# Elementwise x·y with GELU on one core: two 64 KB-row stretches of DRAM in place of three uneven ones, and the opening loads split by operand

## The chip, the cores and the metric

The kernel runs on one core of a Trainium2 chip. The metric is device time in microseconds (us) of one execution; the number for a kernel is the median of its runs.

## The reference

```python
batch, dim = 1024, 4096            # x and y, float32, 16.8 MB each
z = x * y
out = 0.5 * z * (1 + np.tanh(np.sqrt(2 / np.pi) * (z + 0.044715 * z ** 3)))   # float32
```

So 33.55 MB are read, 16.78 MB are written, and each element takes one multiplication and one GELU in its tanh form.

## The kernel before

The work is elementwise, so any element may lie in any partition. The kernel views x, y and out each as one flat run and cuts it into three stretches, `PIECES` (line 14), counted in columns of a 128-partition tile: 0 to 1280, 1280 to 17664, and 17664 to 32768. Inside a stretch, partition p owns one contiguous row of DRAM. A row of the first stretch is 5120 bytes, one of the second 65,536 bytes, and one of the third 60,416 bytes. The whole of x stays in SBUF as `xs` (32,768 columns); products and results are written over it in place. y goes through a smaller buffer `ys` of 20,440 columns, in three loads (`Y_LOADS`, line 16: the first and last column, and where it begins in `ys`).

Every transfer covers 128 partitions and so gives 128 rows, eight to each of the core's 16 DMA engines. In what follows the transfers of before are called by stretch and operand: xA and yA are the 5 KB-row ones, xB and yB the 64 KB-row ones, xC and yC the 60,416-byte ones.

The order in time is written by hand with semaphores:

- SyncE (SP) issues xA and ScalarE (ACT) issues xB. `_hoist` (line 25) puts both issues into the program's first block, ahead of each engine's first drain.
- SP then waits until xA has landed (line 81) and issues yB and xC one after the other.
- SP waits for multiplication 3 (`sem_mul`, line 86), which frees the part of `ys` that yC needs, and issues yC; it waits for multiplication 4 and issues yA.
- VectorE (DVE) multiplies (line 99): four steps of 4096 columns on stretch B, seven of 2048 and one of 768 on stretch C, one of 1280 on stretch A. Ahead of each stretch it waits for x and y of that stretch.
- ScalarE runs one GELU for each multiplication, as soon as that is done (line 107).
- SP issues three stores (line 116): B, after yC has landed (line 114) and the GELUs of B are done; C after the GELUs of C; A after the last GELU.
- Last, SP waits for the first two stores, clears the semaphores and waits for the third (lines 118 to 122).

SP's DMAs go through one queue (q1 in the profile) and ScalarE's through another (q10); both are worked off by the same 16 DMA engines.

Of the kernel before, what the change touches and what calls it, by code (L numbers as in the profile page):

```python
# [1 line left out]

# [4 lines left out]


F32 = mybir.dt.float32
GELU = mybir.ActivationFunctionType.Gelu_apprx_tanh  # L10

PIECES = [(0, 1280), (1280, 17664), (17664, 32768)]

Y_LOADS = [(1280, 17664, 4056), (17664, 32768, 0), (0, 1280, 15104)]

Y_FREE = [0, 3, 4]

STEPS = [[4096] * 4, [2048] * 7 + [768], [1280]]  # L20
STORES = [(1280, 17664), (17664, 32768), (0, 1280)]
Y_BUF = 20440


def _hoist(nc, issued):

    here = nc.cur_bb.bb.instructions
    first = nc.main_func.blocks[0].instructions
    for ins in issued:
        del here[next(k for k, i in enumerate(here) if i is ins or i.name == ins.name)]  # L30
    engine = issued[0].engine
    at = next(
        k
        for k, i in enumerate(first)
        if i.engine == engine and type(i).__name__ == "InstDrain"
    )
    first[at:at] = issued


@with_exitstack  # L40
def kernel(
    ctx: ExitStack,
    tc: tile.TileContext,
    x: bass.AP,
    y: bass.AP,
    out: bass.AP,
):
    nc = tc.nc
    P = nc.NUM_PARTITIONS

    def columns(t, a, b):

        flat = t.flatten_outer_dims().rearrange("r c -> (r c)")
        pa, pb = next(q for q in PIECES if q[0] <= a and b <= q[1])
        return flat[P * pa : P * pb].rearrange("(p c) -> p c", p=P)[:, a - pa : b - pa]


    tc.close()
    tc.compile()

    xs = nc.alloc_sbuf_tensor("xs", [P, PIECES[-1][1]], F32).ap()
    ys = nc.alloc_sbuf_tensor("ys", [P, Y_BUF], F32).ap()
    sem_x = [nc.alloc_semaphore(f"sem_x{i}") for i in range(len(PIECES))]
    sem_y = [nc.alloc_semaphore(f"sem_y{i}") for i in range(len(Y_LOADS))]
    sem_mul = nc.alloc_semaphore("sem_mul")
    sem_act = nc.alloc_semaphore("sem_act")
    sem_o = [nc.alloc_semaphore(f"sem_o{i}") for i in range(len(STORES))]

    def load_x(i, engine=nc.sync):
        a, b = PIECES[i]  # L70
        return engine.dma_start(out=xs[:, a:b], in_=columns(x, a, b)).then_inc(sem_x[i], 16)

    def load_y(i):
        a, b, r = Y_LOADS[i]
        return nc.sync.dma_start(
            out=ys[:, r : r + b - a], in_=columns(y, a, b)
        ).then_inc(sem_y[i], 16)

    _hoist(nc, [load_x(0).ins])
    _hoist(nc, [load_x(1, nc.scalar).ins])  # L80
    nc.sync.wait_ge(sem_x[0], 16)
    load_y(0)
    load_x(2)
    for i in range(1, len(Y_LOADS)):
        if Y_FREE[i]:
            nc.sync.wait_ge(sem_mul, Y_FREE[i])
        load_y(i)

    nc.scalar.wait_ge(sem_x[0], 16)
    n = 0  # L90
    done = {}
    for i, (a, b, r) in enumerate(Y_LOADS):
        for j, (xa, xb) in enumerate(PIECES):
            if xa <= a < xb:
                nc.vector.wait_ge(sem_x[j], 16)
        nc.vector.wait_ge(sem_y[i], 16)  # L96
        c = a
        for w in STEPS[i]:
            nc.vector.tensor_mul(  # L99
                out=xs[:, c : c + w],  # L100
                in0=xs[:, c : c + w],
                in1=ys[:, r + c - a : r + c - a + w],
            ).then_inc(sem_mul, 1)
            n += 1
            done[c + w] = n
            nc.scalar.wait_ge(sem_mul, n)
            nc.scalar.activation(  # L107
                out=xs[:, c : c + w], in_=xs[:, c : c + w], func=GELU
            ).then_inc(sem_act, 1)
            c += w  # L110

    for i, (a, b) in enumerate(STORES):
        if i == 0:
            nc.sync.wait_ge(sem_y[-2], 16)
        nc.sync.wait_ge(sem_act, done[b])
        nc.sync.dma_start(out=columns(out, a, b), in_=xs[:, a:b]).then_inc(sem_o[i], 16)
    for i in range(len(STORES) - 1):
        nc.sync.wait_ge(sem_o[i], 16)
    nums = sorted(s.num for s in [*sem_x, *sem_y, *sem_o[:-1], sem_mul, sem_act])
    assert nums == list(range(nums[0], nums[-1] + 1))  # L120
    nc.sync.sem_clear(range(nums[0], nums[-1] + 1))
    nc.sync.wait_ge(sem_o[-1], 16).then_inc(sem_o[-1], -16)


# [1 line left out]
_INS = ['x', 'y']  # L126
_OUTS = [((1024, 4096), 'float32')]


# [23 lines left out]
```

## Time and profile before

| What | Value |
|---|---|
| Median of 3 runs | 119.82 us (119.6 to 119.83) |
| Profiled execution, first to last instruction (its span) | 118.52 us |
| Median less that span | 1.30 us |
| DVE busy | 35.2 us (30% of the span) |
| ACT busy | 30.9 us (26%) |
| DMA queue q1 (SP), share of 16 engines | 82.3% |
| DMA queue q10 (ACT), share of 16 engines | 16.5% |
| Bytes read and written | 33.55 MB and 16.78 MB, 425 GB/s over the span |

The profile gives the profiled execution's own time as its span; what lies around the span in a timed run is the 1.30 us of the third row. The trace also lists every DMA packet with its start, its duration, its queue and its bytes. A row of a transfer is one packet there, and a 4-byte packet that follows a transfer's rows on an engine is that engine's report to the semaphore.

### The profile page before, as it was taken

The numbers are of one execution on the slowest core, as the hardware profiler recorded it, in microseconds if no ns is written. First come the engines' busy times: TensorE is split into PE (matmuls) and PEld (weight loads), VectorE is DVE, ScalarE is ACT, GpSimd is POOL, SyncE is SP. The second block draws the span as 40 slices with busy tenths as digits, with TensorE's granted clock in tenths as the row PEclk, the third lists the DMA queues.
The fourth block names the chain that finished last, engine by engine and source line by source line (L and its number), as shares of the span: only waits on it lengthen the run. The fifth ranks groups of instructions, "written<-read, shape, count | busy, mean of one in ns | idle before, by whom it ended". The sixth has DMA issues, their size and how long they took to land.

```text
span 118.5 us, 83 instructions
## 1 busy us (share of the span) xinstructions
DVE 35.2 (30%) x13; ACT 30.9 (26%) x14; POOL 0.2 (0%) x4
## 2 busy tenths in 40 slices
DVE  0000000000000069999920000059999940000000
ACT  0000000000000000999975000006998990000000
POOL 0000000000000000000000000000000000000000
DMA  9888899889988897798797797798899887977975
GB/s 492 382 382 382 354 597 464 354 354 465 597 354 354 354 632 347 326 632 347 326 632 347 326 632 347 326 575 354 354 531 531 354 354 326 653 326 326 653 326 221
DMA packets 1296, 50.33 MB, mean 425 GB/s; under 512 B 144, under 2 KB 144, under 8 KB 528
## 3 DMA queue, kind: packets, MB, share of 16 engines
q1 hardware_dynamic: 1152, 41.94, 82.3%
q10 hardware_dynamic: 144, 8.39, 16.5%
HBM read 33.55 MB, written 16.78 MB: 425 GB/s over the span
## 4 chain that ended last, share of the span: by engine, by line
DMA 55%; DVE 24%; ACT 3%; issue 1%; DVEq 0%
DMA ys<-in_y_dram 43%; DVE xs L99 24%; DMA xs<-in_x_dram 11%; ACT xs L107 3%; DVEq L96 0%
## 5 line engine op out<-in xcount | busy, mean ns | idle before, releaser
L99 DVE TENSOR_TENSOR xs<-xs,ys 128x2048 f32<-128x2048 f32 (+3 forms) x13 | 35.2, 2778 | 60.9 <-DMA ys<-in_y_dram 60.9
L107 ACT ACTIVATE xs<-xs 128x2048 f32<-128x2048 f32 (+3 forms) x13 | 29.6, 2300 | 19.6 <-DVE xs L99 19.6
L107 ACT ACT_TABLE_LOAD x1 | 1.3, 1283 | 47.2 <-DVE xs L99 47.2
L137 POOL MEMSET const-uint8-127<- 128x1 uint8 x1 | 0.1, 102 | 0.0
L137 POOL MEMSET const-bfloat16-1.0<- 128x1 bf16 x1 | 0.1, 101 | 0.0
L137 POOL MEMSET const-float32-0.0<- 128x1 f32 x1 | 0.1, 98 | 0.2 <-issue 0.2
L137 POOL MEMSET const-float32-1.0<- 128x1 f32 x1 | 0.1, 98 | 0.0
## 6 DMA issues: line engine op xcount, KB each, us to landing
xs<-in_x_dram SPq DMA_DIRECT2D x1, 7552.0 KB, 46.5
ys<-in_y_dram SPq DMA_DIRECT2D x1, 7552.0 KB, 22.5
out_dram<-xs SPq DMA_DIRECT2D x1, 7552.0 KB, 20.4
xs<-in_x_dram SPq DMA_DIRECT2D x1, 640.0 KB, 13.6
ys<-in_y_dram SPq DMA_DIRECT2D x1, 640.0 KB, 19.7
out_dram<-xs SPq DMA_DIRECT2D x1, 640.0 KB, 20.8
xs<-in_x_dram ACTq DMA_DIRECT2D x1, 30.4
ys<-in_y_dram SPq DMA_DIRECT2D x1, 29.0
```

Of the source, the lines that this page charges most:

```text
L99: nc.vector.tensor_mul(out=xs[:, c : c + w], in0=xs[:, c : c + w], in1=ys[:, r + c - a : r + c - a + w],).then_inc(sem_mul, 1)
L107: nc.scalar.activation(out=xs[:, c : c + w], in_=xs[:, c : c + w], func=GELU).then_inc(sem_act, 1)
L137: nc = _bacc.Bacc("TRN2", target_bir_lowering=False, num_devices=1)
```

## The change

- The flat run is cut into two stretches of 16,384 columns; every DRAM row is 64 KB apart from the next. Call the transfers x0, x1, y0, y1, y2, o0 and o1.
- SP opens with x0 (8.4 MB, 64 KB rows) and ScalarE with y0 (the same size). Both are hoisted. SP issues x1 right behind, without a wait.
- y's second half comes as y1, 12,288 columns (48 KB of each row), after multiplication 3, and y2, 4096 columns (16 KB of each row), after multiplication 4.
- DVE works in four steps of 4096 and eight of 2048 columns, twelve in place of thirteen.
- There are two stores: o0 after y1 has landed and the first four GELUs are done, o1 after the last GELU. Ahead of clearing the semaphores SP also waits for y2.
- ScalarE no longer waits for the first piece of x (line 89 of before).

```diff
-PIECES = [(0, 1280), (1280, 17664), (17664, 32768)]
+HALF = 16384
-Y_LOADS = [(1280, 17664, 4056), (17664, 32768, 0), (0, 1280, 15104)]
+Y_LOADS = [(0, 16384, 4056), (16384, 28672, 0), (28672, 32768, 12288)]
-Y_FREE = [0, 3, 4]
-STEPS = [[4096] * 4, [2048] * 7 + [768], [1280]]
-STORES = [(1280, 17664), (17664, 32768), (0, 1280)]
+STEPS = [[4096] * 4, [2048] * 6, [2048, 2048]]
...
-        pa, pb = next(q for q in PIECES if q[0] <= a and b <= q[1])
-        return flat[P * pa : P * pb].rearrange("(p c) -> p c", p=P)[:, a - pa : b - pa]
+        h = a // HALF * HALF
+        return flat[P * h : P * (h + HALF)].rearrange("(p c) -> p c", p=P)[:, a - h : b - h]
...
     _hoist(nc, [load_x(0).ins])
-    _hoist(nc, [load_x(1, nc.scalar).ins])
-    nc.sync.wait_ge(sem_x[0], 16)
-    load_y(0)
-    load_x(2)
-    for i in range(1, len(Y_LOADS)):
-        if Y_FREE[i]:
-            nc.sync.wait_ge(sem_mul, Y_FREE[i])
-        load_y(i)
+    _hoist(nc, [load_y(0, nc.scalar).ins])
+    load_x(1)
+    nc.sync.wait_ge(sem_mul, 3)
+    load_y(1)
+    nc.sync.wait_ge(sem_mul, 4)
+    load_y(2)
 
-    nc.scalar.wait_ge(sem_x[0], 16)
...
-        for j, (xa, xb) in enumerate(PIECES):
-            if xa <= a < xb:
-                nc.vector.wait_ge(sem_x[j], 16)
+        nc.vector.wait_ge(sem_x[a // HALF], 16)
         nc.vector.wait_ge(sem_y[i], 16)
...
-    for i, (a, b) in enumerate(STORES):
-        if i == 0:
-            nc.sync.wait_ge(sem_y[-2], 16)
+    nc.sync.wait_ge(sem_y[1], 16)
+    for i in range(2):
+        a, b = i * HALF, (i + 1) * HALF
         nc.sync.wait_ge(sem_act, done[b])
         nc.sync.dma_start(out=columns(out, a, b), in_=xs[:, a:b]).then_inc(sem_o[i], 16)
-    for i in range(len(STORES) - 1):
-        nc.sync.wait_ge(sem_o[i], 16)
-    nums = sorted(s.num for s in [*sem_x, *sem_y, *sem_o[:-1], sem_mul, sem_act])
+    nc.sync.wait_ge(sem_o[0], 16)
+    nums = sorted(s.num for s in [*sem_x, *sem_y, sem_o[0], sem_mul, sem_act])
...
+    nc.sync.wait_ge(sem_y[2], 16)
     nc.sync.sem_clear(range(nums[0], nums[-1] + 1))
-    nc.sync.wait_ge(sem_o[-1], 16).then_inc(sem_o[-1], -16)
+    nc.sync.wait_ge(sem_o[1], 16).then_inc(sem_o[1], -16)
```

## The prediction, made blind

> **What bounds the kernel now.** The page's busy times come first: no compute engine is busy for a third of the span, so they bound nothing by their sum.
>
> ```profile
> ## 1 busy us (share of the span) xinstructions
> DVE 35.2 (30%) x13; ACT 30.9 (26%) x14; POOL 0.2 (0%) x4
> ```
>
> Next the windows view, cut where the first DMA packet starts and where the last one ends; its last two columns are the mean busy share of the 16 DMA engines and GB/s.
>
> ```profile
> 0.00:1.00 1.00, 0.00 (x0) 0.00 (x0) 0.20 (x4) 1.00 0.00 0
> 1.00:118.13 117.13, 35.21 (x13) 30.90 (x14) 0.00 (x0) 1.00 1.00 430
> 118.13:118.52 0.39, 0.00 (x0) 0.00 (x0) 0.00 (x0) 1.00 0.00 0
> ```
>
> Between 1.00 and 118.13 us the DMA engines are full. So the chain of waits, which names DVE for 24% of the span, misleads here: while it follows DVE, other rows move. Only three things can change the time: how long the rows take, holes between them, and the 1.01 us before and 0.39 us behind them.
>
> The packet list, followed on one DMA engine, shows rows back to back; a short extract (start us, ns, queue, bytes):
>
> ```
> 1.119 216 q1 5120
> 2.506 2620 q10 65536
> 5.120 196 q1 5120
> 5.315 2418 q10 65536
> 12.947 2422 q10 65536
> 15.366 2418 q10 65536
> 17.780 2418 q1 65536
> 20.194 2418 q10 65536
> ```
>
> From it come the prices, start to start: 2.414 us for a 64 KB load row (17.780 to 20.194), 2.227 for a 60,416-byte one (yet eight of them go from 41.935 to 59.749), 0.193 for a 5 KB one. For stores on that engine: 2.426 (eight from 79.110 to 98.525), 2.231 (eight to 116.377), 0.205 (eight to 118.016). Two queues with rows waiting alternate one row at a time.
>
> Where the holes could come from is in the timeline and in SP's waits:
>
> ```profile
> 42.66 17.43 DVE L99 TENSOR_TENSOR xs<-xs,ys 128x4096 f32<-128x4096 f32 x4 [42.66 <-DMA ys<-in_y_dram]
> 55.79 4.66 SPq L75 DMA_DIRECT2D ys<-in_y_dram  x2
> 78.27 19.77 SPq L116 DMA_DIRECT2D out_dram<-xs  x3
> 78.34 17.78 DVE L99 TENSOR_TENSOR xs<-xs,ys 128x2048 f32<-128x2048 f32 x9 [18.25 <-DMA ys<-in_y_dram]
> ...
> 93.88 3.80 ACT L107 ACTIVATE xs<-xs 128x2048 f32<-128x2048 f32 x3 [0.29 <-DVE xs L99]
> ```
>
> ```profile
> SPq L116 <- DMA ys<-in_y_dram: 14.5, 1, 14.5
> ```
>
> yC is issued at 55.79 while xC still moves until 60, so nothing is lost there. Store B waits 14.5 us for yC, is issued at 78.27, and its first rows start at 79.11, at least 0.84 us later; what covers that is yA's 1.54 us alone. By the packet list nine of the 16 engines run dry here, for 0.1 to 0.5 us; the mean over the engines (yA's ends at 79.04, the store's starts at 79.17) is 0.13 us.
>
> **The change part by part.** The sum is made in DMA time of one engine, of the profiled execution (118.52 us); 1.30 us around the span, from the median 119.82, is carried over.
>
> Rows. Before: 16 rows of 5 KB at 0.193 (3.09), 16 of 64 KB at 2.414 (38.62), 16 of 60,416 at 2.227 (35.63), stores 8 × (2.426 + 2.231 + 0.205) = 38.90; sum 116.24. After: 24 load rows of 64 KB (57.94); y1's 48 KB rows lie on the line between 0.193 and 2.227, 1.812 each (14.50); y2's 16 KB rows by that line 0.607 (4.86); 16 store rows of 64 KB (38.82); sum 116.12. Gain 0.12 us. The bytes are the same; what goes is the part of a row's cost that doesn't shrink with it.
>
> The hole at 79 us. y2 now lasts 8 × 0.607 = 4.9 us, against 0.84 to 0.93 us from the issue of o0 to its rows. Gain 0.13 us on the mean engine. The slowest engine had none, so the bounds are 0 and 0.13; I take 0.13, since the engines' finishes close up during the stores (0.6 us apart at yA's landing, 0.2 at the last store's).
>
> The start. Before, the five 5 KB rows ahead of ScalarE's first row took 1.31 us on the mean engine (first starts at 1.12, that row at 2.43) instead of 5 × 0.193 = 0.97: 0.34 lost. ScalarE's first row took up to 2.858 us, 2.58 in the mean, 0.16 over a later one. After, one first row of 64 KB runs while all others queue. No such row opens before; the nearest is ScalarE's first, 0 to 0.44 over. I take 0.30 as its loss, a gain of 0.50 − 0.30 = 0.20, between 0 and 0.50.
>
> The end. The last report is 0.12 us behind the median engine's with 5 KB rows at the end (118.37, 118.48), and 0.22 with 64 KB rows (store B: 98.95, 99.16). I take 0.07 lost, between 0 and 0.10.
>
> The moved steps, each costed at nothing with its cover:
> - x0 and y0 alternate, so y0 is done after 16 rows: 1.12 + 0.30 + 38.62 = 40.0, landed by 40.4, against 42.57 before. DVE starts 2 us earlier, which by itself is worth nothing.
> - y1 waits for multiplication 3 and is in SP's queue ahead of y2 and o0. 13.1 us behind DVE's start is 53.5, plus at most 2.1 us to its first row (ScalarE's first, issued at 0.12, started at 2.23) is 55.6; x1's rows last until 59.4. Cover 3.8 us; beyond that each late microsecond costs one. y2 follows at 57.8, 16 us ahead of its turn.
> - o0 is issued when y1 lands, about 74.1, behind y2 in the queue, whose rows end at 78.8. Its GELUs are done by 62.
> - o1 waits for the last GELU: DVE from 74.2, eight steps at 2.20 (ACT's start-to-start in the timeline) to 91.8, the GELU behind by 2.2: 94.0. Its rows are needed at 98.2, cover 3.3 us after issue (before, 96.55 plus 0.9 against 98.6).
> - ScalarE's dropped wait and the added wait for y2 at the end stand beside 14 us and 38 us of idle time; nothing is queued behind the latter but the clear, itself 19 us early.
>
> Sum: −0.12 − 0.13 − 0.20 + 0.07 = −0.38, a span of 118.14 and a time of 119.45 us. Outer bounds of the main case: no start or hole gain and a full loss at the end, −0.02 (119.80); all of both and no loss at the end, −0.75 (119.07).
>
> **The rivals.** (1) The start-up gain isn't there: the engines lose the same 0.50 us. Then −0.18, 119.64, within what a measurement of this kernel can tell from no change (about 0.2%, 0.24 us). For it: the excess may be DRAM's first answers, whoever asks.
>
> (2) Slower: a 64 KB opening row comes later than a 5 KB one. SP's 5 KB row started 1.01 us behind its issue, ScalarE's 64 KB row 2.11 us. If the row's size makes that difference, x0 starts 1.1 us later and nothing covers it: 119.45 + 1.1 = 120.55. Against: store B's 64 KB rows came 0.84 us behind their issue, and exactly five 5 KB rows ran ahead of ScalarE's on the mean engine, which looks like rows already taken up. It decides from a first packet later than 1.4 us. [...]
>
> (3) Slower by far: SP's queue gets ahead. x1 now stands right behind x0; if an engine took all 16 of SP's rows first, y0 would end with x1 at 59.4, multiplication 3 at 72.7, y1's rows would come at 73.6, and 14 us of empty DMA would make 133.5. It decides once y0 is over 3.8 us late, two rows. Against: from 13 to 30 us the two queues alternate row by row. [...]
>
> **How the numbers follow.** Main case (start-up gain, over 0.2%) 0.50; rival 1 0.24; rival 2 0.20; rival 3 0.04; anything else slower 0.02. So faster 0.50, same 0.24, slower 0.26. The range goes from 119.15, nearly the main case's best, to 120.55, rival 2; it leaves out rival 3 and the outermost tails. The main case with rival 1 alone is 119.15 to 119.75.
>
> **What would show it.** Right: first packets at 1.0 to 1.4; y0 landed near 40.4 and DVE starting there; rows alternating q1, q10 from the second or third on; no engine idle near 79; o1 issued near 94, landed near 118.1. Wrong: a first packet near 2 us (rival 2), y0 landing at 45 or later (rival 3), idle DMA behind x1 or ahead of o1, or 64 KB rows longer than 2.42 us when both queues read.

## The result, and the profile after

| | Before | After |
|---|---|---|
| Median | 119.77 us (119.6 to 119.83, 4 runs) | 121.09 us (120.83 to 121.13, 4 runs) |
| Span of the profiled execution | 118.52 us | 119.75 us |

The ratio is 1.0107, with a 95% interval of 1.0093 to 1.0121. The change makes the kernel 1.1% slower, 1.3 us. The forecast was 119.45 us, in a range up to 120.55, with slower at 0.26.

The page's busy times, and the windows view cut as the one of before at the first packet's start and the last one's end (last two columns: DMA share, GB/s):

```profile
DVE 35.1 (29%) x12; ACT 31.0 (26%) x13; POOL 0.2 (0%) x4
```

```profile
0.00:1.00 1.00, 0.00 (x0) 0.00 (x0) 0.20 (x4) 1.00 0.00 0
1.00:119.40 118.40, 35.14 (x12) 31.03 (x13) 0.00 (x0) 1.00 1.00 425
119.40:119.76 0.36, 0.00 (x0) 0.00 (x0) 0.00 (x0) 1.00 0.00 0
```

The DMA engines are as full as before (share 1.00), yet carry 425 GB/s in place of 430. Nothing waits for data more than it did (VectorE 57.9 us in all, before 60.9); some packets take longer. So the shares of busy time can't show the loss, and the packet list must.

The timeline after:

```profile
0.00 1.90 SPq L68 DMA_DIRECT2D xs<-in_x_dram  x2
...
41.66 17.43 DVE L91 TENSOR_TENSOR xs<-xs,ys 128x4096 f32<-128x4096 f32 x4 [41.66 <-DMA ys<-in_y_dram]
...
54.79 4.67 SPq L72 DMA_DIRECT2D ys<-in_y_dram  x2
...
75.29 20.10 SPq L108 DMA_DIRECT2D out_dram<-xs  x2
75.37 17.71 DVE L91 TENSOR_TENSOR xs<-xs,ys 128x2048 f32<-128x2048 f32 x8 [16.27 <-DMA ys<-in_y_dram]
...
93.11 1.91 ACT L99 ACTIVATE xs<-xs 128x2048 f32<-128x2048 f32 x1 [0.29 <-DVE xs L91]
```

DVE starts at 41.66 (forecast 40.4), the first store o0 is issued at 75.29 (74.1), and the last GELU ends at 95.0 (94.0). In SP's waits the one of the first store for y is still there:

```profile
SPq L108 <- DMA ys<-in_y_dram: 12.5, 1, 12.5
```

All this is far enough ahead of its use. The windows around the end of the loads show what is not as planned:

```profile
74.10:76.60 2.50, 1.23 (x1) 0.00 (x0) 0.00 (x0) 1.00 1.04 439
76.60:77.90 1.30, 1.30 (x2) 0.21 (x1) 0.00 (x0) 1.00 1.19 365
77.90:79.30 1.40, 1.40 (x1) 1.40 (x1) 0.00 (x0) 1.00 0.79 199
79.30:80.80 1.50, 1.50 (x2) 1.21 (x2) 0.00 (x0) 1.00 2.01 863
```

A packet is counted in the window in which it starts, so single figures swing: the last line has the starts of o0's 64 KB rows. The share counts packets in the same way, so GB/s divided by the share takes that out: the first line gives 422 at a full share, the third 252. The packet list, followed on one engine from y2's fifth row to o0's first (start us, ns, queue, bytes), shows why:

```
76.881 611 q1 16384
77.488 1195 q1 16384
78.680 1001 q1 16384
79.677 611 q1 16384
80.290 2418 q1 65536
```

y2's 16 KB rows that start before 76.5 us take 611 to 620 ns each. The sixth and seventh of an engine's eight take about 1.0 us each in the mean over the 16 engines, and single rows up to 1.27. Together the eight lose 0.95 us.

From the packet list, per engine (means over the 16, and the spread from the first to the last engine):

| | Before | After |
|---|---|---|
| First 16 rows of x by start, mean | 366 ns (5 KB) | 3136 ns (64 KB; later ones 2419) |
| All loads ended | 79.04 (78.74 to 79.44) | 80.23 (79.94 to 80.75) |
| First store's rows start | 79.19 (79.11 to 79.45) | 80.24 (79.94 to 80.76) |
| All rows ended | 118.01 (117.95 to 118.12) | 118.87 (118.58 to 119.39) |

So of 1.24 us of span, 0.86 is a later mean end and 0.41 is spread: the last engine ends 0.52 behind the mean, against 0.11 before. What lies behind the last packet is 0.03 shorter. In the mean end, the loads are 1.19 later; the hole's end returns 0.14, and the stores, which take 38.64 us instead of 38.83, return 0.19.

### The profile page after: what moved, and what is told of

Same layout as the page of the kernel before. It is cut to its first block, busy times and chain, and to the rows that moved or that the text cites. A ratio compares the mean times of both kernels' runs of the same rounds, so it can differ in the third digit from the quotient of the medians.

```text
span 119.8 us, 78 instructions
## 1 busy us (share of the span) xinstructions
DVE 35.1 (29%) x12; ACT 31.0 (26%) x13; POOL 0.2 (0%) x4
## 4 chain that ended last, share of the span: by engine, by line
DMA 52%; DVE 25%; ACT 2%; issue 1%; DVEq 0%
DMA ys<-in_y_dram 52%; DVE xs L91 25%; ACT xs L99 2%; DVEq L88 0%
## 5 line engine op out<-in xcount | busy, mean ns | idle before, releaser
L91 DVE TENSOR_TENSOR xs<-xs,ys 128x2048 f32<-128x2048 f32 (+1 forms) x12 | 35.1, 2998 | 57.9 <-DMA ys<-in_y_dram 57.9
L99 ACT ACTIVATE xs<-xs 128x2048 f32<-128x2048 f32 (+1 forms) x12 | 29.7, 2479 | 62.4 <-DVE xs L91 62.4
```

What stands on the lines that cost most here:

```text
L91: nc.vector.tensor_mul(out=xs[:, c : c + w], in0=xs[:, c : c + w], in1=ys[:, r + c - a : r + c - a + w],).then_inc(sem_mul, 1)
L99: nc.scalar.activation(out=xs[:, c : c + w], in_=xs[:, c : c + w], func=GELU).then_inc(sem_act, 1)
```

## The experiments

In each, "load rows' loss" is the time by which the last load rows exceed their usual duration, in the mean of the 16 engines, from the packet list. Ratios are to the kernel before, measured on the same chip.

**1. Small opening rows.** On the changed kernel:

```diff
-        a, b = i * HALF, (i + 1) * HALF
+        a, b = [(0, 1280), (1280, HALF), (HALF, 2 * HALF)][i]
...
```

> The changed kernel, but x's first half is loaded as two transfers on SyncE's queue: columns 0 to 1280 (5 KB rows) first, columns 1280 to 16384 right behind. Theory 'opening row' (the first packet's size makes the loss: the first 64 KB row took 3.14 us in the mean instead of 2.42): the opening loss falls from 0.72 us to about 0.5 as in the kernel before, the engines' spread at the first half's end falls from 0.75 us, and the time falls by 0.2 to 0.4 us to about 120.8. Rival 'first answers' (whatever comes first pays it): no change, 121.0 to 121.1. Both leave the slow rows of y2 near 77 to 79 us.

Measured: 120.81 us, ratio 1.0085 (1.0057 to 1.0113). The first 5 KB rows took 771 ns instead of 196, and all excess up to 3 us comes to 0.71 us, as with the 64 KB row (0.72). So the packet's size is not what costs. The engines were 0.6 us apart when x's first half and y0 were in, against 0.75. y2's rows still lost 0.74 us. The time is the one that "opening row" had put, but for another reason: the opening lost as much as before, and what shrank is y2's loss, from 0.95 to 0.74 us. Why it shrank isn't shown.

**2. First store after y2 has landed.**

```diff
-    nc.sync.wait_ge(sem_y[1], 16)
+    nc.sync.wait_ge(sem_y[2], 16)
     for i in range(2):
...
```

The wait for y2 at the end of the kernel becomes one for y1.

> The changed kernel, but the first store is issued only once y2 has landed, so no store stands in the queue behind y2 while VectorE multiplies beside it as before. Theory 'queued store' (the store's arrival behind y2 makes y2's rows slow): all of y2's 16 KB rows take 0.61 us, y2 lands near 79.9 instead of 81.1; then the queue is empty for about 0.9 us until the store's rows come, which costs 0.9 us but lets the engines close up (0.8 us apart until then): time 120.6 to 121.0. Rival 'compute beside small rows' (VectorE's and ScalarE's accesses slow them): rows 6 and 7 of y2 still take about 1.0 us, y2 lands at 81.1, and the time is 121.8 to 122.1.

Measured: 121.59 us, ratio 1.0139 (1.0124 to 1.0154). The same windows as above:

```profile
74.10:76.60 2.50, 1.24 (x1) 0.00 (x0) 0.00 (x0) 1.00 0.98 419
76.60:77.90 1.30, 1.30 (x2) 0.21 (x1) 0.00 (x0) 1.00 1.03 441
77.90:79.30 1.40, 1.40 (x1) 1.40 (x1) 0.00 (x0) 1.00 0.79 339
79.30:80.80 1.50, 1.50 (x2) 1.21 (x2) 0.00 (x0) 1.00 0.00 0
80.80:82.30 1.50, 1.50 (x2) 1.21 (x2) 0.00 (x0) 1.00 1.64 699
```

DVE and ACT do the same work at the same time, and no row of y2 is over 619 ns; 77.90 to 79.30 carries 339 GB/s instead of 199, and y2 lands at 80.15 instead of 81.09. So neither compute nor the 16 KB rows were the cause: the waiting store was. The price is the empty line from 79.30 on. The hole (rows end at 79.29, the store's start at 81.07) costs more than the slow rows did, and the time was worse than I expected. But it closes the engines up: the last rows end within 0.15 us of each other.

**3. First store at multiplication 5.**

```diff
     nc.sync.wait_ge(sem_y[1], 16)
+    nc.sync.wait_ge(sem_mul, 5)
```

> The changed kernel, but the first store also waits for multiplication 5 (the first of the second half, which ends near 77.7), so its rows come near 78.6 instead of 76.2. Theory 'queued store': y2's rows 5 to 7 take 0.61 us, only the last of the slow engines can suffer, no hole of note; y2 lands near 80.0 and the time is about 120.1 to 120.4. Rival 'compute beside small rows': y2 lands at 81.1 and the time stays at 121.0 to 121.1.

Measured: 120.08 us, ratio 1.0018 (1.0004 to 1.0032). The store is issued at 78.01, 1.8 us ahead of the loads' end, and y2's last four rows take 611 ns. There is no hole either: 0.9 of the 1.1% is gone with one wait. (The profiled execution was the longest of its kind, 120.62 us, with rows up to 0.2 us too long between 59 and 76 us, well ahead of the store's issue; their cause is not known.)

**4. The opening alone, in the kernel before.**

```diff
-    _hoist(nc, [load_x(0).ins])
-    _hoist(nc, [load_x(1, nc.scalar).ins])
-    nc.sync.wait_ge(sem_x[0], 16)
-    load_y(0)
-    load_x(2)
+    _hoist(nc, [load_x(1).ins])
+    _hoist(nc, [load_y(0, nc.scalar).ins])
+    load_x(2)
+    load_x(0)
...
```

As in the change itself, ScalarE's wait for the first piece of x goes too.

> The kernel before with the opening of the changed one alone: SyncE opens with x's 64 KB-row stretch, ScalarE with y's, then x's other two stretches follow without a wait; y's two later loads and the three stores are those of before. Theory 'opening row': the first row takes about 3.1 us, the loads end 0.2 to 0.3 us later than in the kernel before, the hole at 79 us closes the engines' spread, and the time is 119.9 to 120.1, so that most of the 1.3 us of the change lies elsewhere. Rival 'the opening is all of it': 120.8 to 121.1.

Measured: 120.11 us, ratio 1.0015 (1.0006 to 1.0025). The first row took 3088 ns, the loads ended at 79.30 instead of 79.04, and the hole brought the engines together (the first store's rows end from 98.71 to 98.86). The opening is worth 0.2 us of the 1.3.

**5. The store early, behind 48 KB rows.**

```diff
-Y_LOADS = [(0, 16384, 4056), (16384, 28672, 0), (28672, 32768, 12288)]
+Y_LOADS = [(0, 16384, 4056), (16384, 20480, 0), (20480, 32768, 4096)]
-STEPS = [[4096] * 4, [2048] * 6, [2048, 2048]]
+STEPS = [[4096] * 4, [2048] * 2, [2048] * 6]
```

> The changed kernel with y's second half split the other way: the 4096 columns first (16 KB rows), the 12288 columns second (48 KB rows). The first store then is issued near 65 us and stands in the queue behind 48 KB rows, which run to about 79 us. Theory 'a passing disturbance' (a store's arrival behind loads slows them for some 2 us, from 1.9 us after its issue): one or two 48 KB rows near 67 to 69 us lose about 1 us in the mean, all loads land near 81.0, time 120.9 to 121.2. Rival 'as long as a store is queued': the rows stay slow until the loads end, over 5 us more, time over 125. Second rival 'small rows alone suffer': no 48 KB row is over 1.9 us, loads land near 80.0, time 120.0 to 120.3.

Measured: 120.86 us, ratio 1.0089 (1.0076 to 1.0103). None of the three was right as put. The store is issued at 65.46 and waits in the queue for over 14 us:

```profile
66.30:77.10 10.80, 3.73 (x2) 3.82 (x2) 0.00 (x0) 1.00 1.01 437
77.10:77.80 0.70, 0.00 (x0) 0.00 (x0) 0.00 (x0) 1.00 3.87 1123
77.80:79.70 1.90, 0.00 (x0) 0.00 (x0) 0.00 (x0) 1.00 0.00 0
```

For 10.8 us the loads run at 437 GB/s, undisturbed. Then the eighth and last 48 KB row, started between 77.2 and 77.7 on all engines, takes 2708 ns instead of 1815. DVE and ACT are idle from 77.1 to 79.7, so compute is out again. The disturbance is not tied to the store's issue at 65.46, but to the last load row ahead of it, over 11 us later: here it is a price of the turn from loads to a store that is already queued, 0.89 us.

**6. The first store in two, 5 KB rows first.**

```diff
-    for i in range(2):
-        a, b = i * HALF, (i + 1) * HALF
+    for i, (a, b) in enumerate([(0, 1280), (1280, HALF), (HALF, 2 * HALF)]):
...
```

> The changed kernel, but the first store is issued as two: columns 0 to 1280 (5 KB rows) first, columns 1280 to 16384 right behind, at the same moment as the first store of the changed kernel. Theory 'read ahead' (the engine begins with the queued 64 KB store row while y2's rows still come, so a 5 KB row would disturb less): y2's rows lose under 0.4 us in the mean instead of 0.98, time 120.3 to 120.6. Rival 'the arrival itself, whatever its rows': the same 0.9 to 1.0 us, time 121.0 to 121.3.

Measured: 121.02 us, ratio 1.0103 (1.0087 to 1.0118); y2's rows lost 0.93 us, with 64 KB rows 0.95. The size of the waiting store's first row made no difference. "Read ahead" in this form fell.

**7. Small opening rows and multiplication 5 together.**

```diff
-        a, b = i * HALF, (i + 1) * HALF
+        a, b = [(0, 1280), (1280, HALF), (HALF, 2 * HALF)][i]
...
     nc.sync.wait_ge(sem_y[1], 16)
+    nc.sync.wait_ge(sem_mul, 5)
```

> The 5 KB opening load of x and the first store waiting for multiplication 5, together, on the changed kernel. If the two costs add (0.2% and 0.9% of the time), the ratio to the kernel before is 0.998 to 1.001, 119.7 to 120.0 us. Theory 'what is left is the opening': the engines' spread of 0.5 us remains to the end, and the kernel isn't faster than before by more than 0.2%.

Measured: 120.10 us, ratio 1.0030 (1.0019 to 1.0041). No load row was slow and there was no hole, but the gain of edit 1 did not come on top of edit 3; the two intervals of 3 and 7 overlap. The excess up to 3 us was 0.62 us, again that of a 64 KB opening. So what run 1 gained was not the opening's.

**8. Adjacent 5 KB rows first, the rest of the opening as changed.** On the kernel before:

```diff
-    _hoist(nc, [load_x(1, nc.scalar).ins])
-    nc.sync.wait_ge(sem_x[0], 16)
-    load_y(0)
+    _hoist(nc, [load_y(0, nc.scalar).ins])
+    load_x(1)
     load_x(2)
...
```

Here too ScalarE's wait for the first piece of x goes.

> The kernel before, its opening changed alone: SyncE opens with the 5 KB-row stretch of x (rows next to each other in DRAM, as before) and queues x's other two stretches right behind it without a wait; ScalarE opens with y's 64 KB-row stretch. Theory 'spread rows' (5 KB pieces of rows 64 KB apart opened with 0.77 us a row, adjacent 5 KB rows with 0.37): the first rows take 0.35 to 0.40 us, time 119.8 to 119.9. Rival 'two streams' (x and y read at once, or the queue behind, make the first answers late): first rows of about 0.75 us, time 120.0 to 120.1.

Measured: 119.76 us, ratio 0.9996 (0.9987 to 1.0005). First rows of 378 ns, all excess up to 3 us 0.40. Reading x and y at once and queueing behind the opening cost nothing. Over all runs, adjacent 5 KB rows lost 0.18 to 0.48 us up to 3 us, and openings with rows 64 KB apart, of 5 KB or 64 KB, 0.58 to 0.78.

**9 and 10. A long cover in the kernel before, the store timed or early.** The C stretch of y in two loads, so that 4.9 us of load rows follow the load that the store waits for:

```diff
-Y_LOADS = [(1280, 17664, 4056), (17664, 32768, 0), (0, 1280, 15104)]
+Y_LOADS = [(1280, 17664, 4056), (17664, 29952, 0), (29952, 32768, 12288), (0, 1280, 15104)]
...
-            nc.sync.wait_ge(sem_y[-2], 16)
+            nc.sync.wait_ge(sem_y[1], 16)
+            nc.sync.wait_ge(sem_mul, 5)
...
```

The last line shown is in run 9 alone. Multiplications keep their widths, and SP also waits for the last two loads of y behind its stores.

> The kernel before with stretch C of y loaded in two (12288 and 2816 columns), the 5 KB-row load of y last as before, and the first store issued at multiplication 5, near 77.4 us, about 1.7 us ahead of the end of the loads. Theory 'the turn' (a store that comes to the queue some 2 us ahead of the last load row costs nothing and leaves no hole): loads end near 79.0 in the mean with no slow row, the store follows at once, the last row ends at 117.7 in the mean with the engines 0.3 to 0.6 us apart, time 119.6 to 119.75 against 119.8 of before. Rival 'the hole was free' (the slowest engine sets the end): 119.75 to 119.95.

> The same kernel without the wait for multiplication 5: the first store is issued when the 12288 columns have landed, near 75 us, 4 us ahead of the end of the loads, as in the changed kernel, while the opening, the row widths and the three stores are those of the kernel before. Theory 'the turn': the last load rows lose 0.9 to 1.0 us in the mean and the engines stay 0.6 us apart, time 120.7 to 121.0. Rival 'it needs the 64 KB rows or the y load of 16 KB rows': 119.7 to 120.0.

Measured: run 9 119.83 us, ratio 1.0004 (0.9995 to 1.0012); run 10 120.89 us, ratio 1.0093 (1.0079 to 1.0107). SP's issues of the stores, and the windows, run 9's first:

```profile
77.26 17.46 SPq L117 DMA_DIRECT2D out_dram<-xs  x3
```

```profile
74.83 19.77 SPq L116 DMA_DIRECT2D out_dram<-xs  x3
```

```profile
76.90:78.40 1.50, 1.50 (x2) 1.19 (x1) 0.00 (x0) 1.00 0.95 399
78.40:80.08 1.68, 1.68 (x2) 1.39 (x2) 0.00 (x0) 1.00 1.75 752
```

```profile
76.90:78.40 1.50, 1.50 (x2) 1.17 (x1) 0.00 (x0) 1.00 0.96 254
78.40:80.08 1.68, 1.68 (x2) 1.39 (x2) 0.00 (x0) 1.00 0.90 216
```

The only difference is when SP issues the first store, at 77.26 or at 74.83. In run 9 the loads end at 79.00 and the stores follow in the second window; in run 10 the last 11 and 5 KB rows lose 1.22 us and no store has started by 80.08. So the step that costs can be put into the kernel before, without the two stretches, the 64 KB opening or the two stores, and gives 0.9% there. Run 9 also settles what the hole at 79 us was worth. Without it the mean end came 0.33 us earlier (117.69), but the engines stayed 0.47 us apart, and the time is that of before.

**11. The short cover in the changed kernel.**

```diff
-Y_LOADS = [(0, 16384, 4056), (16384, 28672, 0), (28672, 32768, 12288)]
+Y_LOADS = [(0, 16384, 4056), (16384, 31488, 0), (31488, 32768, 15104)]
-STEPS = [[4096] * 4, [2048] * 6, [2048, 2048]]
+STEPS = [[4096] * 4, [2048] * 7 + [768], [1280]]
```

> The changed kernel with y's second half split as 15104 and 1280 columns (59 KB and 5 KB of each row) in place of 48 KB and 16 KB, so that the first store is issued 1.5 us ahead of the loads' end as in the kernel before; all else is the changed kernel's. Theory 'the turn': no slow load row, a short hole near 79 us that closes the engines up, and of the 1.3 us only the opening's part is left: 120.0 to 120.15. Rival 'the two stretches and two stores themselves cost': 120.6 to 121.0.

Measured: 120.13 us, ratio 1.0033 (1.0022 to 1.0044). No slow load row, a hole from 79.22 to 79.46, and rows ending from 118.24 to 118.39. From 1.0107 to 1.0033 by the split of y alone, with the multiplication widths that go with it.

**12. The store 2.8 us ahead.** On the kernel of run 3:

```diff
-STEPS = [[4096] * 4, [2048] * 6, [2048, 2048]]
+STEPS = [[4096] * 4, [1024, 3072] + [2048] * 4, [2048, 2048]]
```

> The changed kernel with the first store waiting for multiplication 5, as in the run that waits for it, but multiplication 5 has 1024 columns and the next 3072, so the store is issued near 76.6 us, 2.7 us ahead of the loads' end: between the leads that cost nothing (1.7 to 1.8 us) and those that cost 0.7 to 1.2 us (4 us and more). Theory 'what counts is the last 48 KB or so of load rows behind which the store's rows wait' (the store's rows come 0.9 us behind the issue, so 1.8 us ahead of the end): part or all of the loss, 0.4 to 0.9 us, time 120.5 to 121.0. Rival 'a store needs over 3 us in the queue to disturb': no slow row, 120.0 to 120.2.

Measured: 120.32 us, ratio 1.0049 (1.0032 to 1.0066); y2's rows lost 0.14 us. Part of the loss, but less than I had put.

The runs in one table. The lead is from the first store's issue to the mean end of the loads:

| Run | Lead, us | Load rows' loss, us | Ratio |
|---|---|---|---|
| 2 | -0.9 | 0 | 1.0139 |
| 11 | 0.7 | 0 | 1.0033 |
| before | 0.8 | 0 | 1 |
| 4 | 0.8 | 0 | 1.0015 |
| 8 | 0.8 | 0 | 0.9996 |
| 9 | 1.7 | 0 | 1.0004 |
| 3 and 7 | 1.8 | 0 | 1.0018, 1.0030 |
| 12 | 2.8 | 0.14 | 1.0049 |
| after | 4.9 | 0.95 | 1.0107 |
| 1 | 4.9 | 0.74 | 1.0085 |
| 6 | 5.1 | 0.93 | 1.0103 |
| 10 | 5.5 | 1.22 | 1.0093 |
| 5 | 14.7 | 0.89 | 1.0089 |

In run 3 this is y2's last four rows; the slow rows well ahead of the store are left out. Up to a lead of 1.8 us the last load rows lose nothing; at 4.9 and beyond they lose 0.7 to 1.2 us, and the loss doesn't grow with the lead. No version was measurably faster than the kernel before (the lowest ratio, run 8's 0.9996, has 1 inside its interval).

## Why the prediction was wrong

**The step that failed** is "o0 is issued when y1 lands, about 74.1, behind y2 in the queue", costed at nothing because y2's 4.9 us cover the 0.9 us from the issue to the first row. The cover held, and no engine ran dry. But I took a queue as free of side effects for what stands ahead in it. The store waiting there took 0.95 us from y2's last rows. The trace of before couldn't show that: its store came 0.8 us ahead of the loads' end, behind eight 5 KB rows, which took 196 ns each. I had sought a price for waiting too short and none for waiting too long; the step needed a bound on both sides, and the nearest row, store C issued 2 us ahead of store B's end, is a store behind a store. Runs 2, 5, 9 with 10, and 11 show it from four sides. None of the prediction's signs of being wrong was a slow load row ahead of a store, and its 0.26 for slower stood almost wholly on rivals 2 and 3, neither of which happened.

Term by term, in us of the profiled execution:

| Term | Forecast | Measured |
|---|---|---|
| y2's last rows, slowed by the waiting store | 0 | +0.95 |
| Rows at their usual durations | -0.12 | -0.23 (loads 0.04, stores 0.19) |
| Hole at 79 us, mean engine | -0.13 | -0.14 |
| Start | -0.20 | +0.29 (0.22 slow rows, 0.07 later first packets) |
| End: last engine against the mean, and what follows it | +0.07 | +0.38 |
| Sum | -0.38 | +1.25 (the spans differ by 1.24) |

**The hole** was costed as a gain of 0.13 us, with 0 as the other bound because "The slowest engine had none". On the mean engine the gain came, but in the kernel's time run 9 shows none, so that bound was the right one; and the prediction missed more: at the hole the engines that are ahead wait (before, the loads ended over 0.70 us, from 78.74 to 79.44, and the store's rows started over 0.34 us, from 79.11 to 79.45). With it gone, the opening's spread of 0.75 us lasted to the end (0.81), and the last engine's distance from the mean rose by 0.41 us. I had put 0.07 for the end. In run 9 hole and spread balance.

**The start** was costed as a gain of 0.20 us and was a loss. The first 64 KB row exceeded a later one by 0.72 us, not 0.30; the whole loss of before was 0.50. That is worse than rival 1, which had the same 0.50. The engines' first packets came at 1.01 to 1.62 us (mean 1.19, against 1.12 before). One of the 16 is past the 1.4 that was to decide for rival 2, the others came by 1.39; a start 1.1 us late did not happen, and the row was long rather than late. y0's rows ended at 40.55 in the mean and at 41.01 on the last engine, against a forecast of 40.0, and DVE started 1.3 us later than forecast; the DMA engines stayed full meanwhile (share 1.04 from 1 to 41 us), so that cost nothing by itself. Run 4 gives the opening's share of the time, 0.15%. Run 8 (0.40 us up to 3 us) and the 5 KB openings of runs 1 and 7 (0.71 and 0.62) point to rows 64 KB apart as the reason.

**What held.** The row sum: 24 rows of 64 KB at 2.414 us start to start, y1's at 1.812 and y2's undisturbed ones at 0.607, as put. Two queues alternating row by row: turns were of one 64 KB row all through the opening, 2.42 us each, y0's last row ended 2.42 us, one turn, behind x0's in the mean, and rival 3 did not occur. The covers of y1, y2 and o1 were ample: issued at 54.79, 59.12 and 95.04, their rows started 5.1, 15.3 and 4.5 us later in the mean. 64 KB store rows without a hole ahead took 2.414 us instead of 2.426, which the sum had not foreseen; the stores became 0.19 us shorter.

**How the 1.07% splits.** Taking the early store back gives 0.74 points (run 11) or 0.89 (run 3); putting it into the kernel before costs 0.93 (run 10). The opening alone costs 0.15 (run 4), which is about what run 3 leaves. Run 11 keeps 0.33: besides the opening, its hole is longer (0.24 us against 0.14), because the store is issued 0.88 us behind the mean end of the y load that it waits for, in the kernel before 0.77; and it has a second hole of 0.05 us ahead of o1. That these two make up the rest was not tested.

**Open.** What inside a DMA engine makes the last load rows slow while a store waits was not settled. In these runs it is bound to the last 48 KB or so of an engine's loads ahead of a queued store (after: rows 5 to 8 of y2 took 0.66, 1.04, 1.06 and 0.63 us in the mean; run 5: the last 48 KB row), on all 16 engines (after: 0.45 to 1.43 us each), whatever the rows' sizes (5, 11, 16 or 48 KB; store rows of 5 or 64 KB). Waiting in a queue alone does not do it: in the changed kernel y2 stands queued for 15 us behind y1, whose last rows take 1815 ns as always, and o1 for 4.5 us behind o0, whose rows take 2418. Of the orders seen here, only a store behind loads did it. Where the loss sets in between leads of 1.8 and 4.9 us is known from one run alone, and a store on ScalarE's queue was not tried.

## What to carry to other kernels

When DMA engines are full, look at the durations of single packets at each change of direction: a share of 1.00 hid rows that ran at half speed here (1195 ns in place of 611). Issue a store so that its rows arrive in about the last microsecond of the loads ahead of it in the queue (here it was issued 1.7 to 1.8 us ahead of their end, and in run 2 rows started 0.9 us behind the issue), neither after their end (run 2, 1.0139) nor long before (run 10, 1.0093); a semaphore of the compute that runs there anyway can time it. A small hole may be free (0.14 us in the kernel before, none in run 9, ratio 1.0004), where it lets engines that have drifted apart start together again, so price it on the slowest engine and not on the mean.

## What the runs showed of the hardware that I had not expected

- A store queued 4.9 us or more ahead of the end of the loads made their last rows lose 0.7 to 1.2 us; queued 1.7 to 1.8 us ahead, nothing (the table of the runs).
- Engines that were 0.75 us apart when the first loads were in were 0.81 apart at the end where no engine ran dry, and closed up to 0.15 us where there was one hole (after, run 2).
- Store rows of 64 KB took 2.414 us start to start where they followed loads without a hole, and about 2.425 behind one (after, run 2: 118.87 − 80.24 and 119.85 − 81.07 over 16 rows).
- Opening loads whose rows lie 64 KB apart lost 0.58 to 0.78 us in the first 3 us over all runs, adjacent 5 KB rows 0.18 to 0.48.
